# A trunk layer on one core: value weights of eight heads side by side, thirteen instead of ten seven-product pairs in the last matrix, and sums of its weights kept in DRAM

## The chip, the cores and the metric

The kernel runs on one core of one Trainium2 chip. The time is device microseconds of one execution of the whole layer. The kernel before takes 1129.91 us, the median of three runs from 1128.61 to 1129.95.

## The reference

One layer on x of 256 rows by 2048, in float32, with float32 weights. What the change touches is the value part of the first projection and the last product of the feed-forward part.

```python
h   = RMSNorm(x);  q, k, v = h @ w_in               # 16 heads of 128
o   = 8 stick-breaking heads | 8 dilated heads, each RMS-normalised
x   = x + RMSNorm(o @ w_out)                        # 2048 -> 2048
h   = RMSNorm(x)
u   = h @ w_up                                      # 2048 -> 2 x 5504
u   = sum(up[:, j:j + S] * conv_w[j] for j in range(3)) + conv_b
y   = gelu(gate) * val                              # 5504
out = x + RMSNorm(y @ w_down)                       # 5504 -> 2048
```

## The kernel before

**Weights.** All of them are float32 in DRAM and are used once. A chunk is 128 rows by 2048 columns, 1 MB, and is loaded by SP's queue in two pieces of 128x1024 (512 KB, function load, L78) into five slots called raw that go round: a load waits on SP until the slot's last reader is done, and everything behind it on SP waits with it. Each piece is split in two: ACT casts it to a rounded high part (wh, L88), VectorE (DVE) subtracts this from the piece and gets the low part (wl, L93; called "its low" below). Four buffers each hold wh and wl. TensorE (PE) then makes three matmuls of a product: high of the data by high of the weights, low by high, high by low. Loads run two chunks ahead of PE, the splits one.

**Order of chunks.** Four times: the four value chunks of four heads (kind "v", 2 PSUM banks), then eight chunks of queries and keys ("qk"). Then 16 chunks of "out", 86 of "up", and down. The first chunks are written out by hand: x comes transposed in pieces (load_x, L209) between the weights, and split_x makes its two parts. x for the residual, the tables and the parameters are loaded before chunks 4 to 7 (the table named between). The attention of each head runs in four or five steps beside the following chunks, its PSUM in the pool ps_at; chunks use ps_mm. A scheduler sets each engine's order from the program, except where pin keeps the written one (start, end, and the passage from out to up).

**Down.** y has 43 blocks of 128 columns of y (row blocks of w_down). The output is made in two halves of 1024 columns (cp 0 and 1), each in eight PSUM banks, numbered 1 to 8 by what is summed in them. A single row block takes four products (2 blocks of 128 rows of x by 2 blocks of 512 columns). A pair of row blocks is a 2x2 by 2x2 block product in seven products in the manner of Winograd; the weights' side needs the units T13 (two products), T24 (two), Rb (two, the plain blocks b11 and b22) and Ra (one, the plain block b21). With b12, b21 and [b11|b22] loaded, T13 is [b12|b12] + [b11|b22] (L542), and the two halves of T24 are the first of T13 plus b22 (L543) and this plus b21 (L544). Each unit then has its cast and its low, three units ahead of PE (AHEAD). The data's side (seven sums of y for each pair) is made during up in convolved. There are ten pairs and 23 singles, in the order of _down_plan: of the first half two singles, then a pair and one or two singles in turn, four singles at the end; of the second half the same without the two. The last four singles of the second half (HELD) are worked through bank by bank, and the final normalisation runs beside them, its order pinned: close adds a bank to its sum, rows.mean and newton make the row's factor, put multiplies, adds x and stores.

Of the kernel before, what the change touches and what calls it, by code (L numbers as in the profile page):

```python
# [9 lines left out]
F32 = mybir.dt.float32  # L10
# [6 lines left out]
P = 128  # L17
# [15 lines left out]

NPAIR = 10
HELD = 4
# [16 lines left out]
def layer_kernel(ctx: ExitStack, tc: tile.TileContext, a, out: bass.AP):  # L52
# [137 lines left out]
    A.preload_act_table_set("natural_log_exp_and_others")  # L190
    gpre = cpool.tile([P, KT], F32, name="gpre")
    par = cpool.tile([P, P_END], F32, name="par")
# [5 lines left out]
    apool = phA.__enter__()  # L198
    cst = apool.tile([P, C_END - P], F32, name="cst", bufs=1)
    x1 = apool.tile([P, 2, D], F32, name="x1", bufs=1)  # L200
    x1_kept = nc.dram_tensor("x1_kept", (S, D), F32, kind="Internal").ap()
# [18 lines left out]
    nc.scalar.dma_start(gpre, a["par"][:, P_PRE:P_PRE + KT])  # L220
    warm = cpool.tile([P, 512], BF16, name="warm")
# [4 lines left out]
    w0 = chunks[0][3]  # L226
# [11 lines left out]
    split_x(1, 2)  # L238
    parts_of[0] += split(raws[0][1:2])
    split_x(2, 4)  # L240
    parts_of[0] += split(raws[0][2:3])
    nc.scalar.dma_start(ident, a["cst"][:, C_ID:C_END])
    for i in range(1, 4):
        load_x(4 * i, 4 * i + 4)
        raws[i] = load(chunks[i][3], chunks[i][4])
        split_x(4 * i, 4 * i + 4)
        if i == 1:
            parts_of[1] = split(raws[1])
    between[4] = (x1[:, 0, :], a["x"][0:P, :])
    between[5] = (x1[:, 1, :], a["x"][P:S, :])  # L250
    between[6] = (cst, a["cst"][:, 0:C_ID])
    between[7] = (par, a["par"])

# [133 lines left out]
    class Rows:  # L387
# [6 lines left out]
        def squares(self, ps, t, c):  # L394
            jk = wpool.tile([P, 512], BF16, tag="jks", name="jks", bufs=1)
            jk = jk[:, 0:ps.shape[-1]]
            pin(A.activation(jk, ps, AF.Square, accum_out=self.ss[:, t, c:c + 1]))
# [50 lines left out]
    def convolved(ps, p, s):  # L448
# [4 lines left out]
        V.tensor_tensor(u, u, r2B, op=ALU.mult)  # L453
        cv = phB.tile([P, S], F32, tag=f"cv{s}", name="cv")
        A.activation(cv, u, AF.Identity, scale=cw(2), bias=par[:, P_CB + f:P_CB + f + 1])  # L455
        V.scalar_tensor_tensor(cv[:, 1:], u[:, :S - 1], cw(1), cv[:, 1:], op0=ALU.mult, op1=ALU.add)
        V.scalar_tensor_tensor(cv[:, 2:], u[:, :S - 2], cw(0), cv[:, 2:], op0=ALU.mult, op1=ALU.add)
        if s == 0:
            A.activation(cv, cv, AF.Gelu_apprx_tanh)
            gate[0] = cv  # L460
        else:
            m, odd = p // (FT // NPAIR), p % (FT // NPAIR)
            if p in SINGLES:
                n = SINGLES.index(p)
                V.tensor_tensor(cv, gate[0], cv, op=ALU.mult)
                A.copy(yt[0][:, n, :], cv)
                V.tensor_tensor(yt[1][:, n, :], cv, yt[0][:, n, :].bitcast(F32), op=ALU.subtract)
                return
            if odd == 0:
                pair[0] = phB.tile([P, 8, P], F32, tag="pair", name="pair", bufs=1)  # L470
# [12 lines left out]
    class Down:  # L483
# [6 lines left out]
        PAIR = (  # L490
            ("T13", ((5, 3, 0), (7, 5, 512))),
            ("T24", ((6, 4, 0), (4, 2, 512))),
            ("Rb", ((1, 0, 0), (3, 6, 512))),
            ("Ra", ((2, 1, 0),)),
        )
        ONE = ((4, 1, 0), (3, 0, 512), (2, 0, 0), (8, 1, 512))

        def __init__(self):
            self.units, self.tiles = [], []
            for cp in range(2):  # L500
                at = 0
                for kind, j in _down_plan(cp):
                    first = len(self.tiles)
                    n = 2 if kind == "pair" else 1
                    for _ in range(n):
                        self.tiles.append(a["w_dn"][cp, :, at:at + 1024])
                        at += 1024
# [5 lines left out]
            self.raws, self.parts, self.sums = [], [], {}  # L513
            self.left = {}
# [5 lines left out]
            self.begun = set()  # L520

        def load(self, n):
            while len(self.raws) < min(len(self.tiles), n):
                raw = wpool.tile([P, HALF], F32, tag="raw", name="raw", bufs=RAW_BUFS, padded_shape=[P, HALF])
                nc.sync.dma_start(raw, self.tiles[len(self.raws)])
                self.raws.append(raw)

        def prepare(self, n):
            while len(self.parts) < min(len(self.units), n):
                cp, what, j, first, _ = self.units[len(self.parts)]  # L530
                self.load(first + 5)
                ra = self.raws[first]
                if what == "one":
                    src = ra
                else:
                    rb = self.raws[first + 1]
                    if what == "T13":
                        t13, t24 = room[:, 3, 0:HALF], room[:, 3, HALF:]
                        self.sums = {"T13": t13, "T24": t24, "Rb": rb, "Ra": ra[:, 512:]}
                        b12 = ra[:, 0:512].rearrange("p (o c) -> p o c", o=1).broadcast_to([P, 2, 512])  # L540
                        two = lambda x: x.rearrange("p (o c) -> p o c", o=2)
                        V.tensor_tensor(two(t13), b12, two(rb), op=ALU.add)  # L542
                        V.tensor_tensor(t24[:, 0:512], t13[:, 0:512], rb[:, 512:], op=ALU.add)  # L543
                        V.tensor_tensor(t24[:, 512:], t24[:, 0:512], ra[:, 512:], op=ALU.add)  # L544
                    src = self.sums[what]
                self.parts.append(low(src, high(src)))
# [38 lines left out]
        def run(self):  # L585
# [66 lines left out]
            r = rows.newton(*mean)  # L652
            for lo, hi in ((0, 256), (256, 1024), (1024, 1536), (1536, 2048)):
                put(1, lo, hi, r)
            pinned[0] = False

    down = Down()
    for i, (kind, p, s, _, w) in enumerate(chunks):
        parts = ahead(i, 0 if (kind, p, s) == ("out", 3, 3) else SPLITS)
        if kind == "v":  # L660
            if s == 0:
                mm["v"] = [ps_mm.tile([P, 512], F32, tag="mm", name="mmv") for _ in range(2)]
            mm_moving(mm["v"], parts, hT[0], hT[1], 4 * s, s == 0, s == 3)
            if s == 3:
                late = LATE if p == 0 else 0
        if kind in ("v", "qk") and late is not None:
            if late == 0:
                g = p // 4 if kind == "qk" else p
                if g == 0:
                    first_norm()  # L670
                vts[g] = apool.tile([P, 2, 512], F32, tag="vt", name="vt")
                for t in range(2):
                    A.activation(vts[g][:, t, :], mm["v"][t], AF.Copy, scale=rstd1[:, t:t + 1])
                late = None
# [229 lines left out]
```

## Time and profile before

| | |
|---|---|
| median of the runs | 1129.91 us (1128.61 to 1129.95) |
| profiled execution, its own time | 1130.5 us |
| its span | 1128.7 us |
| granted clock | 0.998 |
| PE, DVE, ACT busy | 99%, 76%, 57% |
| bytes moved | 216.86 MB, 192 GB/s over the span |
| attention and out, up, down | to about 400, 414 to 893, 894 to 1120 us |

PE is what the traces call TensorE's matmuls, PEld its loading of stationary data, which overlaps; DVE is VectorE, ACT ScalarE, POOL GpSimd, and SP the engine whose queue issues nearly all DMAs. Rows of a timeline read: start, duration, engine, line, operation, output<-input, shapes, number of instructions that were merged in the row, and in brackets how long the engine had been idle before and for whom it had waited. Busy time of a matmul is longer than the step from one to the next, since they overlap; steps are read from starts. A group's row gives the sum and the mean of one in ns.

### The profile page before, as it was taken

To read this page: it belongs to the slowest core of one execution; us is meant where nothing else is said; L and a number is where in the kernel's file an instruction comes from. 1 tells how busy PE (TensorE), PEld (TensorE's weight loads), DVE (VectorE), ACT (ScalarE), POOL (GpSimd) and SP (SyncE) were. 2 spreads that over 40 slices of the span, in tenths; PEclk is the share of its full clock that TensorE was granted. 3 is DMA by queue.
4 is the path that set the end of the run, shared out by engine and by line. 5 is a ranking of instruction groups with operands and counts; after the bars stand their busy time and mean duration, and the time that the engine had idled before them with its cause. 6 is when DMAs were issued, how large, how long until landed. Compare 5 with 4: busy or idle time off the path is not lost.

```text
span 1128.7 us, 16033 instructions
## 1 busy us (share of the span) xinstructions
PE 1112.2 (99%) x5873; PEld 945.2 (84%) x5873; DVE 857.0 (76%) x1340; ACT 646.6 (57%) x1039; POOL 3.6 (0%) x10
## 2 busy tenths in 40 slices
PE   8999999999999989999999999999999999999996
PEld 6888888888888878888888888888888878877885
DVE  6665565766765489788888887888888898888987
ACT  7555564655654386555555555555555555554653
POOL 0000000000000000000000000000000000000000
PEclk9999999999999999999999999999999999999999
DMA  9764545545555556555555555555555555555555
GB/s 357 251 209 164 180 157 168 168 155 181 166 169 188 187 186 206 186 187 187 186 188 187 187 189 186 188 186 189 187 188 187 162 206 205 205 199 205 202 198 204
DMA packets 59695, 216.86 MB, mean 192 GB/s; under 512 B 6753, under 2 KB 7393, under 8 KB 58849
## 3 DMA queue, kind: packets, MB, share of 16 engines
q1 hardware_dynamic: 59328, 215.77, 57.4%
q8 instruction: 46, 0.75, 0.3%
q14 instruction: 33, 0.26, 0.1%
q10 hardware_dynamic: 288, 0.07, 0.0%
HBM read 211.63 MB, written 4.19 MB: 191 GB/s over the span
## 4 chain that ended last, share of the span: by engine, by line
PE 95%; DVE 2%; ACT 1%; DMA 1%; issue 0%; SPq 0%; DVEq 0%; ACTq 0%
PE mmu L101 28%; PE mmu L104 14%; PE mmqk L101 10%; PE p L563 6%; PE p L561 6%; PE p L562 6%; PE mmqk L104 5%; PE mmo L138 3%; PE mmo L134 3%; PE mmo L135 3%; PE mmv L134 3%; PE mmv L135 2%; PE mmv L138 2%; DVE wl L93 1%; DMA mg<-in_xT 1%; PE mmu L111 1%
## 5 line engine op out<-in xcount | busy, mean ns | idle before, releaser
L93 DVE TENSOR_TENSOR wl<-raw,wh 128x1024 fp32r<-128x1024 f32 (+1 forms) x387 | 457.9, 1193 | 202.4 <-ACT wh L88 199.7
L88 ACT CAST wh<-raw 128x1024 fp32r<-128x1024 f32 (+1 forms) x387 | 394.4, 1027 | 342.7 <-PE mmu L101 194.5
L101 PE MATMUL mmu<-hT,wh 128*128 128x512 f32 x1344 | 340.6, 395 | 0.2 <-ACT wh L88 0.2
L101 PEld LDWEIGHTS mmu<-hT,wh 128*128 128x128 f32 x1344 | 240.8, 188 | 45.0 <-ACT wh L88 0.4
L104 PEld LDWEIGHTS mmu<-hT,wl 128*128 128x128 f32 x1344 | 184.1, 188 | 15.3
L104 PE MATMUL mmu<-hT,wl 128*128 128x256 f32 x1344 | 187.4, 282 | 0.0
L101 PE MATMUL mmqk<-hT,wh 128*128 128x512 f32 x512 | 132.9, 400 | 0.0
L101 PEld LDWEIGHTS mmqk<-hT,wh 128*128 128x128 f32 x512 | 92.0, 188 | 17.1
L88 ACT CAST wh<-room 128x1024 fp32r<-128x1024 f32 x40 | 42.0, 1050 | 71.1 <-DVE room L542 49.5
L104 PEld LDWEIGHTS mmqk<-hT,wl 128*128 128x128 f32 x512 | 70.0, 188 | 5.8
L561 PE MATMUL p<-wh,yt 128*128 128x512 f32 (+1 forms) x188 | 72.9, 388 | 0.0
L562 PE MATMUL p<-wh,yt 128*128 128x512 f32 (+1 forms) x188 | 72.9, 388 | 0.0
L563 PE MATMUL p<-wl,yt 128*128 128x512 f32 (+1 forms) x188 | 72.5, 386 | 0.2 <-DVE wl L93 0.2
L104 PE MATMUL mmqk<-hT,wl 128*128 128x256 f32 x512 | 71.2, 281 | 0.0
L561 PE MATMUL p<-wh,yp 128*128 128x512 f32 x140 | 55.2, 395 | 0.4 <-ACT wh L88 0.4
L563 PE MATMUL p<-wl,yp 128*128 128x512 f32 x140 | 54.6, 394 | 0.5 <-DVE wl L93 0.5
L562 PE MATMUL p<-wh,yp 128*128 128x512 f32 x140 | 55.0, 393 | 0.0
L134 PE MATMUL mmv<-wh,hT 128*128 128x512 f32 x128 | 51.7, 405 | 1.6 <-ACT wh L88 1.3
L455 ACT ACTIVATE cv<-u,par 128x256 f32<-128x256 f32 x86 | 51.4, 598 | 2.1 <-DVE u L453 2.1
L93 DVE TENSOR_TENSOR wl<-room,wh 128x1024 fp32r<-128x1024 f32 x40 | 48.9, 1222 | 4.4 <-ACT wh L88 3.6
L135 PE MATMUL mmv<-wh,hT 128*128 128x512 f32 x128 | 50.7, 396 | 0.3 <-DVE hT L236 0.3
L134 PE MATMUL mmo<-wh,mix 128*128 128x512 f32 x128 | 50.6, 396 | 0.0
(175 smaller groups left out, 1219.1 us busy)
## 6 DMA issues: line engine op xcount, KB each, us to landing
raw<-in_w_up SPq DMA_DIRECT2D x172, 512.0 KB, 4.4
raw<-in_w_dn SPq DMA_DIRECT2D x86, 512.0 KB, 4.3
raw<-in_w_qk SPq DMA_DIRECT2D x64, 512.0 KB, 3.7
raw<-in_w_o SPq DMA_DIRECT2D x32, 512.0 KB, 3.6
raw<-in_w_v SPq DMA_DIRECT2D x31, 512.0 KB, 3.8
x<-in_x SPq DMA_DIRECT2D x2, 1024.0 KB, 9.3
x_kept<-x SPq DMA_DIRECT2D x2, 1024.0 KB, 4.4
x1b<-x_kept SPq DMA_DIRECT2D x4, 512.0 KB, 5.4
```

Source lines behind the costliest of these rows:

```text
L88: pin(A.copy(wh, raw))
L93: pin(V.tensor_tensor(wl, raw, wh.bitcast(F32), op=ALU.subtract))
L101: T.matmul(ps, wh[:, j * P:(j + 1) * P], h[:, k, :, :], start=(k == 0), stop=False, skip_group_check=True)
L104: T.matmul(ps[:, 0, :], wl[:, j * P:(j + 1) * P], h[:, k, 0, :], start=False, stop=(k == KT - 1), skip_group_check=True)
L111: T.matmul(ps[:, 0, :], w[:, k % 8 * P:(k % 8 + 1) * P], h[:, k, 0, :], start=(k == 0 and w is parts[0][0]), stop=False, skip_group_check= ...
L134: T.matmul(ps[t], hi[:, k, tc_], ws, start=(first and i == 0 and j == 0), stop=False)
L135: T.matmul(ps[t], lo[:, k, tc_], ws, start=False, stop=False)
L138: T.matmul(ps[t], hi[:, k, tc_], wl[:, j * 512:(j + 1) * 512], start=False, stop=(last and i == len(parts) - 1 and j == n - 1))
L455: A.activation(cv, u, AF.Identity, scale=cw(2), bias=par[:, P_CB + f:P_CB + f + 1])
L561: T.matmul(ps, yh, wh[:, cs], start=key not in self.begun, stop=False)
L562: T.matmul(ps, yl, wh[:, cs], start=False, stop=False)
L563: T.matmul(ps, yh, wl[:, cs], start=False, stop=self.left[key] == 0)
```

## The change

1. **Pairs.** NPAIR goes from 10 to 13, so there are 17 singles. In down there is now one single between two pairs (none behind pairs 0 and 6 of the first half). On the data's side one of the eight sums is written in place, so that seven lie together and take one cast and one subtraction instead of two each; the row numbers in PAIR follow.
2. **Sums ahead of time.** A new function, presum, makes T13 of all 26 pair tiles during attention and out, one per two chunks, from chunk 8 to 61: SP loads b12 (256 KB) and [b11|b22] (512 KB), two chunks later DVE adds them, one chunk after that SP stores the sum (512 KB) in DRAM (t13_kept). Down loads T13 from there, and [b11|b22] and b21 (256 KB) from the weights: three tiles for a pair instead of two, and no sum of T13 in down. The two sums of T24 go to alternate halves of the last quarter of room.
3. **Start.** The value chunks of the first two groups of four heads alternate, with the second group's PSUM taken from ps_at, then come the 16 query and key chunks of eight heads. The loads of x, the tables and the parameters move from chunks 4 to 7 to chunks 8 to 11. The vectors vt of both groups are made together.
4. **End.** The put of 512 columns of row block 0 is cut in two with rows.mean between, and the last multiplication by the gain (take9) moves behind the first two puts of row block 1.
5. **Buffers.** Some tiles go to other pools or to single buffers (gpre, warm, u, cv, jks).

```diff
-NPAIR = 10
+NPAIR = 13
...
-        u = pool.tile([P, S], F32, tag=name, name=name)
+        u = pool.tile([P, S], F32, tag=name, name=name, bufs=1)
...
-    for g in range(4):
+    for gs in ((0, 1), (2,), (3,)):
         for kq in range(4):
-            chunks.append(("v", g, kq, a["w_v"][g, kq], 2048))
-        for h in range(4 * g, 4 * g + 4):
+            for g in gs:
+                chunks.append(("v", g, kq, a["w_v"][g, kq], 2048))
+        for h in range(4 * gs[0], 4 * gs[-1] + 4):
...
     raws[0] += load(w0[:, 0:512], 512)
     load_x(0, 2)
     raws[0] += load(w0[:, 512:1024], 512)
+    raws[1] = load(w1[:, 0:1024], 1024)
     load_x(2, 4)
     raws[0] += load(w0[:, 1024:], 1024)
+    raws[1] += load(w1[:, 1024:], 1024)
...
-    between[4] = (x1[:, 0, :], a["x"][0:P, :])
+    between[8] = (x1[:, 0, :], a["x"][0:P, :])
...
-                a11, a21, a12, a22, s1, s2, s3, s4 = (y[:, j, :] for j in range(8))
+                a11, a21, a12, a22, s1, s2, s4 = (y[:, j, :] for j in range(7))
                 V.tensor_tensor(s1, a22, a21, op=ALU.subtract)
-                V.tensor_tensor(s3, a11, a21, op=ALU.subtract)
+                V.tensor_tensor(a21, a11, a21, op=ALU.subtract)
...
-                for dst, src in ((slice(0, 1), slice(0, 1)), (slice(1, 7), slice(2, 8))):
-                    A.copy(yp[0][:, m, dst, :], y[:, src, :])
-                    V.tensor_tensor(yp[1][:, m, dst, :], y[:, src, :], yp[0][:, m, dst, :].bitcast(F32), op=ALU.subtract)
+                A.copy(yp[0][:, m, :, :], y)
+                V.tensor_tensor(yp[1][:, m, :, :], y, yp[0][:, m, :, :].bitcast(F32), op=ALU.subtract)
...
+                    if kind == "pair":
+                        self.tiles += [kept[cp, j], a["w_dn"][cp, :, at + 1024:at + 2048], a["w_dn"][cp, :, at + 512:at + 1024]]
+                        self.presums.append((a["w_dn"][cp, :, at:at + 512], self.tiles[-2], kept[cp, j]))
...
+        def presum(self, tick):
+            pair, odd = divmod(tick, 2)
+            if odd and self.summed and tick > 2:
+                t13, _, kept = self.summed.pop(0)
+                nc.sync.dma_start(kept, t13)
+            if not odd and self.summed:
+                t13, one, _ = self.summed[0]
+                b12 = one.rearrange("p (o c) -> p o c", o=1).broadcast_to([P, 2, 512])
+                two = t13.rearrange("p (o c) -> p o c", o=2)
+                V.tensor_tensor(two, b12, two, op=ALU.add)
+            if not odd and pair < len(self.presums):
+                one, two, kept = self.presums[pair]
+                b12 = apool.tile([P, 512], F32, tag="b12", name="b12")
+                nc.sync.dma_start(b12, one)
+                t13 = apool.tile([P, HALF], F32, tag="t13", name="t13")
+                nc.sync.dma_start(t13, two)
+                self.summed.append((t13, b12, kept))
...
-                        V.tensor_tensor(two(t13), b12, two(rb), op=ALU.add)
+                    rb, b21 = self.raws[first + 1], self.raws[first + 2]
+                    if what == "T24":
+                        t24 = room[:, 3, j % 2 * HALF:(j % 2 + 1) * HALF]
                         V.tensor_tensor(t24[:, 0:512], t13[:, 0:512], rb[:, 512:], op=ALU.add)
-                        V.tensor_tensor(t24[:, 512:], t24[:, 0:512], ra[:, 512:], op=ALU.add)
+                        V.tensor_tensor(t24[:, 512:], t24[:, 0:512], b21, op=ALU.add)
...
-            put(0, 1536, 2048, r)
+            put(0, 1536, 1792, r)
             mean = rows.mean(1, 5)
+            put(0, 1792, 2048, r)
+            r = rows.newton(*mean)
+            put(1, 0, 256, r)
+            put(1, 256, 1024, r)
             pin(take9(V))
...
+        if 8 <= i < 62:
+            down.presum(i - 8)
...
+                pool, tag = (ps_at, "at") if p == 1 else (ps_mm, "mm")
+                mm["v", p] = [pool.tile([P, 512], F32, tag=tag, name="mmv") for _ in range(2)]
```

What the scheduler makes of it shows in the order of instructions. First DVE in down, around a pair in the middle of the first half; before, L542 to L544 are the three sums, "wl<-room" the lows of T13 and T24, "wl<-raw" those of Rb, Ra (128x512) and the singles:

```order
L542 TENSOR_TENSOR room<-raw 128x1024
L543 TENSOR_TENSOR room<-room,raw 128x512
L544 TENSOR_TENSOR room<-room,raw 128x512
L93 TENSOR_TENSOR wl<-room,wh 128x1024 x2
```

and after the change, with the sums of T24 at L569 and L570 and T13 read from a raw slot:

```order
L569 TENSOR_TENSOR room<-raw 128x512
L570 TENSOR_TENSOR room<-room,raw 128x512
L93 TENSOR_TENSOR wl<-room,wh 128x1024
L93 TENSOR_TENSOR wl<-raw,wh 128x1024
L93 TENSOR_TENSOR wl<-raw,wh 128x512
L93 TENSOR_TENSOR wl<-raw,wh 128x1024 x2
L569 TENSOR_TENSOR room<-raw 128x512
L570 TENSOR_TENSOR room<-room,raw 128x512
```

The low of T24 now always stands straight behind its own second sum; before, the low of T13 stood between in most pairs. Between one pair's second sum and the next pair's first stand five lows: T24, Rb, Ra, the single and the next T13.

Second PE, in the same place after the change: p6, p4, p1 and p3 are PSUM banks, L588 is high by high, L589 low by high, L590 high by the weights' low. T24 feeds banks 6 and 4, Rb 1 and 3.

```order
L588 MATMUL p6_9005<-wh_9262,yp0_4084 128x512
L589 MATMUL p6_9005<-wh_9262,yp1_4085 128x512
L588 MATMUL p4_9007<-wh_9262,yp0_4084 128x512
L589 MATMUL p4_9007<-wh_9262,yp1_4085 128x512
L588 MATMUL p1_9006<-wh_9269,yp0_4084 128x512
L589 MATMUL p1_9006<-wh_9269,yp1_4085 128x512
L590 MATMUL p6_9005<-wl_9264,yp0_4084 128x512
L590 MATMUL p4_9007<-wl_9264,yp0_4084 128x512
```

The two matmuls by T24's low stand behind six by high parts; before, each stood right behind the two of its own bank.

Third SP at the start, before and then after. x in pieces is mg<-in_xT.

```order
L78 DMA raw<-in_w_v 128x512
L209 DMA mg<-in_xT 128x512
L78 DMA raw<-in_w_v 128x512
L209 DMA mg<-in_xT 128x512
L78 DMA raw<-in_w_v 128x1024
L209 DMA mg<-in_xT 128x1024
```

```order
L78 DMA raw<-in_w_v 128x512
L210 DMA mg<-in_xT 128x512
L78 DMA raw<-in_w_v 128x512
L78 DMA raw<-in_w_v 128x1024
L210 DMA mg<-in_xT 128x512
L78 DMA raw<-in_w_v 128x1024 x2
```

A piece of weights of the second group comes ahead of the second piece of x.

More of the change, by code (lines that the diff above doesn't have):

```diff
@@ L244, in layer_kernel @@
         load_x(4 * i, 4 * i + 4)
-        raws[i] = load(chunks[i][3], chunks[i][4])
+        for j in range(2 * i, 2 * i + 2):
+            raws[j] = load(chunks[j][3], chunks[j][4])
         split_x(4 * i, 4 * i + 4)
         if i == 1:
-            parts_of[1] = split(raws[1])
-    between[4] = (x1[:, 0, :], a["x"][0:P, :])
-    between[5] = (x1[:, 1, :], a["x"][P:S, :])
-    between[6] = (cst, a["cst"][:, 0:C_ID])
-    between[7] = (par, a["par"])
+            parts_of[2] = split(raws[2])
+    between[8] = (x1[:, 0, :], a["x"][0:P, :])
+    between[9] = (x1[:, 1, :], a["x"][P:S, :])
+    between[10] = (cst, a["cst"][:, 0:C_ID])
+    between[11] = (par, a["par"])
     negones = apool.tile([P, P], F32, name="negones", bufs=1)
@@ L469, in convolved @@
             if odd == 0:
-                pair[0] = phB.tile([P, 8, P], F32, tag="pair", name="pair", bufs=1)
+                pair[0] = phB.tile([P, 7, P], F32, tag="pair", name="pair", bufs=1)
             y = pair[0]
@@ L531, in prepare @@
                 self.load(first + 5)
-                ra = self.raws[first]
+                t13 = self.raws[first]
                 if what == "one":
-                    src = ra
+                    src = t13
                 else:
[L536 to L542, printed above, removed]
+                    rb, b21 = self.raws[first + 1], self.raws[first + 2]
+                    if what == "T24":
+                        t24 = room[:, 3, j % 2 * HALF:(j % 2 + 1) * HALF]
                         V.tensor_tensor(t24[:, 0:512], t13[:, 0:512], rb[:, 512:], op=ALU.add)
-                        V.tensor_tensor(t24[:, 512:], t24[:, 0:512], ra[:, 512:], op=ALU.add)
-                    src = self.sums[what]
+                        V.tensor_tensor(t24[:, 512:], t24[:, 0:512], b21, op=ALU.add)
+                        self.t24 = t24
+                    src = {"T13": t13, "T24": self.t24, "Rb": rb, "Ra": b21}[what]
                 self.parts.append(low(src, high(src)))
@@ L648, in run @@
             put(0, 1280, 1536, r)
[L649 removed]
+            put(0, 1536, 1792, r)
             mean = rows.mean(1, 5)
+            put(0, 1792, 2048, r)
+            r = rows.newton(*mean)
+            put(1, 0, 256, r)
+            put(1, 256, 1024, r)
             pin(take9(V))
[L652 to L654 removed]
+            put(1, 1024, 1536, r)
+            put(1, 1536, 2048, r)
             pinned[0] = False
@@ L659, in layer_kernel @@
         parts = ahead(i, 0 if (kind, p, s) == ("out", 3, 3) else SPLITS)
+        if 8 <= i < 62:
+            down.presum(i - 8)
         if kind == "v":
             if s == 0:
[L662 to L665, printed above, removed]
+                pool, tag = (ps_at, "at") if p == 1 else (ps_mm, "mm")
+                mm["v", p] = [pool.tile([P, 512], F32, tag=tag, name="mmv") for _ in range(2)]
+            if i == 0:
+                pass
+            elif i == 1:
+                for half in range(2):
+                    for g in range(2):
+                        some = parts_of[g][2 * half:2 * half + 2] if g == 0 and half == 0 else parts_of[g][half - 2:][:1]
+                        mm_moving(mm["v", g], some, hT[0], hT[1], 2 * half, half == 0, False)
+            else:
+                mm_moving(mm["v", p], parts, hT[0], hT[1], 4 * s, s == 0, s == 3)
+            if s == 3 and p > 0:
+                late = LATE if p == 1 else 0
         if kind in ("v", "qk") and late is not None:
             if late == 0:
-                g = p // 4 if kind == "qk" else p
-                if g == 0:
+                gs = (0, 1) if kind == "qk" else (p,)
+                if gs == (0, 1):
                     first_norm()
-                vts[g] = apool.tile([P, 2, 512], F32, tag="vt", name="vt")
-                for t in range(2):
-                    A.activation(vts[g][:, t, :], mm["v"][t], AF.Copy, scale=rstd1[:, t:t + 1])
+                for g in gs:
+                    vts[g] = apool.tile([P, 2, 512], F32, tag="vt", name="vt")
+                    for t in range(2):
+                        A.activation(vts[g][:, t, :], mm["v", g][t], AF.Copy, scale=rstd1[:, t:t + 1])
                 late = None
```

32 lines of the change are left out of this document (18 added, 14 removed).

## The prediction

> **What bounds the kernel now.** I began with the totals of the page and the share of the chain of waits by engine.
>
> ```profile
> span 1128.7 us, 16033 instructions
> PE 1112.2 (99%) x5873; PEld 945.2 (84%) x5873; DVE 857.0 (76%) x1340; ACT 646.6 (57%) x1039; POOL 3.6 (0%) x10
> PE 95%; DVE 2%; ACT 1%; DMA 1%; issue 0%; SPq 0%; DVEq 0%; ACTq 0%
> ```
>
> TensorE is busy 99% of the span and holds 95% of the chain. So the time can fall in two ways only: fewer matmuls, or less of the little idling that is left. Next came the stages, one window each (length, busy time of PE, its weight loads, DVE, ACT and POOL, granted clock, DMA share, GB/s).
>
> ```profile
> 0.00:20.00 20.00, 16.90 (x61) 10.75 (x62) 12.96 (x22) 13.78 (x23) 0.86 (x7) 1.00 0.90 332
> 14.00:20.00 6.00, 6.00 (x27) 4.82 (x27) 6.00 (x9) 5.75 (x11) 0.00 (x0) 1.00 1.03 425
> 20.00:60.00 40.00, 39.80 (x213) 33.50 (x212) 26.37 (x42) 23.88 (x33) 0.51 (x1) 1.00 0.79 286
> 110.00:157.00 47.00, 47.00 (x280) 41.50 (x279) 28.34 (x47) 26.22 (x49) 0.00 (x0) 1.00 0.52 168
> 205.00:236.00 31.00, 31.00 (x186) 27.37 (x185) 22.27 (x50) 20.50 (x49) 0.00 (x0) 1.00 0.52 167
> 424.00:890.00 466.00, 466.00 (x2650) 406.81 (x2649) 381.73 (x626) 270.57 (x417) 0.00 (x0) 1.00 0.58 189
> 894.00:1120.00 226.00, 224.84 (x985) 182.09 (x983) 202.79 (x220) 127.25 (x150) 1.18 (x1) 1.00 0.57 198
> ```
>
> Attention and up leave PE no gap, up with DVE at 82% (381.73 of 466). Idle time is left in the first 20 us and in down, where DVE is at 90% (202.79 of 226). The clock is full throughout. The list of what PE waited for names the releasers: the first row is of 0 to 20 us, the others of down.
>
> ```profile
> PE mmv L134 <- ACT wh L88: 1.3, 2, 0.7
> PE p L563 <- DVE wl L93: 0.8, 2, 0.5
> PE p L561 <- ACT wh L88: 0.4, 2, 0.3
> ```
>
> **The change part by part.** The sum is made against the profiled execution, 1130.5 us (span 1128.7 and 1.8 around it); the median shown is 1129.91, 0.6 lower.
>
> *Eighteen matmuls less.* Three more pairs, each with seven products for eight, two column halves, three matmuls a product: 18. The price is from the chain, which gives each matmul of 512 columns the same step, and the length of down from its first and last matmul.
>
> ```profile
> 1116.79 0.23 PE p L562
> 1117.03 0.23 PE p L563
> L561 PE MATMUL p<-wh,yt x188: 279/392/398, 893.8 to 1119.6; 128*128 128x512 f32 x180, 128*128 128x256 f32 x8
> L563 PE MATMUL p<-wl,yt x188: 276/388/505, 894.3 to 1119.8; 128*128 128x512 f32 x180, 128*128 128x256 f32 x8
> ```
>
> 18 x 0.23 = **-4.1 us**. Down now has 328 products of three matmuls, 24 of these matmuls at half width: 972 full widths, 223.6 us, in a stretch from 893.8 to 1119.9 (the last start and half a step), 226.1. So PE loses **2.5 us** to waits in down.
>
> *Waits in down.* This is the term that decides. DVE sets the pace of a pair, as its timeline shows.
>
> ```profile
> 962.73 1.22 DVE L93 TENSOR_TENSOR wl<-room,wh 128x1024 fp32r<-128x1024 f32 x1
> 963.87 0.69 DVE L544 TENSOR_TENSOR room<-room,raw 128x512 f32<-128x512 f32 x1
> 965.75 1.23 DVE L93 TENSOR_TENSOR wl<-room,wh 128x1024 fp32r<-128x1024 f32 x1 [1.19 <-ACT wh L88]
> 966.89 4.09 DVE L93 TENSOR_TENSOR wl<-raw,wh 128x1024 fp32r<-128x1024 f32 x4
> 971.86 1.23 DVE L542 TENSOR_TENSOR room<-raw 128x1024 f32<-128x1024 f32 x1 [0.88 <-DMA raw<-in_w_dn]
> 973.12 0.69 DVE L543 TENSOR_TENSOR room<-room,raw 128x512 f32<-128x512 f32 x1
> 973.85 0.69 DVE L544 TENSOR_TENSOR room<-room,raw 128x512 f32<-128x512 f32 x1
> L542 DVE TENSOR_TENSOR room<-raw 128x1024 f32<-128x1024 f32 x20 | 24.5, 1223 | 11.7 <-DMA raw<-in_w_dn 10.2 <-PE mmu L104 1.5
> L93 DVE TENSOR_TENSOR wl<-raw,wh 128x512 fp32r<-128x512 f32 x22 | 15.1, 688 | 0.0
> ```
>
> By starts, a full low takes 1.14 (962.73 to 963.87), the first T24 sum 0.73 (973.12 to 973.85). Where the second sum has its cast straight behind it, as it always will, 1.88 pass up to the low (963.87 to 965.75), 1.19 of it waiting for ACT. A half low takes 0.69 less the 0.09 by which busy time exceeds the step of a full one: 0.60. A pair and one single then cost DVE 0.73 + 1.88 + T24 1.14 + Rb 1.14 + Ra 0.60 + single 1.14 + T13 of the next 1.14 = **7.77 us**. PE needs 33 matmuls, 7.59. DVE is behind by 0.18 a step. A pair without a single (pairs 0 and 6 of the first half) costs 6.62 against 21 matmuls, 4.83. Before, most pairs had two singles (45 matmuls, 10.35), and DVE's longer pair (1.23 more for L542, and 10.2 us over twenty pairs waiting for a DMA) had room beside it. The first half runs eleven steps between pair 1 and the last, ten of 7.77 and one of 6.62, 84.3, where PE has 80.7; less 0.3 of slack from the singles ahead, PE waits 3.3. The second half starts with some 1.7 of slack (a single is 2.76 for PE and 1.14 for DVE, and the first half ends on four; how far DVE may run ahead is limited by four buffers) and takes 86.0 where PE has 83.5: 0.8. Together 4.1 for 2.5: **+1.6**. Bounds: no wait left, -2.5; and 0.15 more a step over 22 steps, +4.9. I take the sum of the rows, nearest to the work.
>
> *One tile more a pair, loaded late.* The order on SP gives the block b21 the slot that Rb frees. From the end of Rb's low to the second sum of the next pair DVE has 0.60 + 1.14 + 1.14 + 0.69, about 3.5 us. The nearest rows are a 512 KB tile in such a slot, from its issue to the instruction that waited for it, and the landing times of down's loads.
>
> ```profile
> 978.12 0.33 SPq L525 DMA_DIRECT2D raw<-in_w_dn  x1
> 981.61 1.23 DVE L542 TENSOR_TENSOR room<-raw 128x1024 f32<-128x1024 f32 x1 [0.64 <-DMA raw<-in_w_dn]
> DMA to landing us min/median/max: 3.3/4.3/6.4
> ```
>
> 3.49 us for 512 KB; 256 KB fewer at 425 GB/s (first windows) is 0.6 less, 2.9: **0**. Bounds: 0, and a tile that takes the median's 4.3 less 0.6, 0.2 late in each of 22 steps, 4.4. I take 0: its like took 3.49, not 4.3. The Trainium skill, DMA: Bandwidth & Descriptors, section "Latency and other measured facts", speaks against it: it gives HBM access as 0.2 us on average and 2 us at high load. By that, an estimate, 2.9 could become 4.7, 1.2 us late. The landings of down, 3.3 to 6.4 for one size, agree that the spread is of that order.
>
> *Sums made in attention.* 26 adds of 1.22 (L542's mean) are 31.8 us of DVE over some 340, 9 points on top of 60% (28.34 of 47) to 72% (22.27 of 31); up ran at 82% without a gap. The bytes, 768 KB read and 512 KB written a pair, 34 MB in all, add 100 GB/s to 168; in 14 to 20 us the queues moved 425 GB/s while PE was busy 6.00 of 6.00. Each add stands two chunks behind its loads and one ahead of its store, so neither DVE nor SP, behind which the weights wait, should stop. **0**; if that cover fails, a store that holds SP costs up to a DVE step, 0.25 of PE for each of 26, **+6.5**.
>
> *Start.* PE's two long waits:
>
> ```profile
> 6.12 0.62 ACT L88 CAST wh<-raw 128x512 fp32r<-128x512 f32 x1 [0.59 <-DMA raw<-in_w_v]
> 8.72 1.05 ACT L88 CAST wh<-raw 128x1024 fp32r<-128x1024 f32 x1 [1.07 <-DMA raw<-in_w_v]
> 8.72 0.39 PE L138 MATMUL mmv<-wl,hT 128*128 128x512 f32 x1
> 9.82 0.50 PE L134 MATMUL mmv<-wh,hT 128*128 128x512 f32 x1 [0.70 <-ACT wh L88]
> 12.25 0.63 PE L138 MATMUL mmv<-wl,hT 128*128 128x512 f32 x2
> 13.48 0.50 PE L134 MATMUL mmv<-wh,hT 128*128 128x512 f32 x1 [0.60 <-ACT wh L88]
> ```
>
> 8.72 + 0.23 to 9.82 is 0.87; 12.25 + two steps to 13.48 is 0.77; 1.64 in all. After the change the next 512 KB of weights need no new x. Between 6.12 and 8.72 landed 768 KB, so 512 KB take 1.73: there at 7.85, cast by 8.90, and PE is free at 8.95. From then on each x piece feeds two groups. I leave 0.2 of the waits: **-1.45** (bounds 0, if x comes as late, and -1.64). x1 and the tables come four chunks later; they are what the 425 GB/s carried without a gap.
>
> *Up.* Pairs, row sums and single buffers add under 10 us to DVE's 381.73 of 466, so at most 84%: **0**, hidden behind PE.
>
> *Tail.*
>
> ```profile
> 1120.45 1.13 DVE L620 SCALAR_TENSOR_TENSOR room<-room,rs,x1p 128x256 f32<-128x256 f32 x2
> 1121.50 0.15 DVE L407 TENSOR_SCALAR_CACHE_REDUCE rj<-ssd 128x5 f32<-128x5 f32 x1
> 1121.58 0.42 DVE L583 TENSOR_TENSOR room<-room 128x256 f32<-128x256 f32 x1
> 1122.61 2.74 DVE L620 SCALAR_TENSOR_TENSOR room<-room,rs,x1b 128x256 f32<-128x256 f32 x4
> ```
>
> The mean (L407) stands behind a put of half the width, some 0.25 earlier, but the multiply by the gain (L583), which was covered by ACT's logarithm, now stands among the last puts, 0.4: **+0.15** (bounds -0.25 and +0.4).
>
> Sum: -4.1 + 1.6 + 0 + 0 - 1.45 + 0 + 0.15 = **-3.8**: 1126.7 by the profiled execution, **1126.1** by the median.
>
> **The rivals.** *PE alone sets down* (waits fall to 0.5, -2.0 for +1.6): 1122.5. For it: 10.2 us of DVE's waits on DMA go, and AHEAD = 3 units of lead absorb single late steps. Against: a lead is spent when every step is 0.18 long, and 7.77 came from rows without a semaphore's extra. *DVE's step is longer than the rows say*, by 0.15 (a T24 cast queued behind another on ACT, a single's load): 22 x 0.15 = 3.3, 1129.4, no measurable change. For it: nothing is left to cover ACT's cast, and PE issues T24's lows six matmuls behind its highs. Against: ACT is at 56% in down (127.25 of 226). *The late b21*: from a landing above 3.5 us DVE stops in each step; half a microsecond late is 22 x 0.5 = 11 us, 1137, slower. For it: the landings of 3.3 to 6.4. Against: half the bytes. *The store in attention holds the weights back*: +6.5, 1132.6, slower. For it: SP sends in order. Against: the add is done a chunk before. That the start's order does nothing is a rival of the start term alone: 1127.5, inside the forecast's own range.
>
> **How the numbers follow.** Forecast 0.44, PE alone 0.14, longer step 0.24, late b21 0.10, store 0.08. 0.2% of 1130 is 2.3 us, about what a measurement can tell: faster is below 1127.6. The forecast and PE alone are faster, but of the forecast 0.02 lies above that bound: 0.56. The longer step and that 0.02 make 0.26 the same; the last two 0.18 slower. The forecast's own range is 1124 to 1128. The whole range begins where no wait is left in down and the start gains all (-4.1 - 2.5 - 1.64 + 0.15, 1121.8) and takes in the store's 1132.6; outside is the late tile alone.
>
> **What would show it.** In the changed profile: 18 matmuls fewer in down; PE's waits for L88 in the first 15 us below 0.3 in all; DVE above 95% busy or waiting for casts from pair to pair with a period near 7.8 us, and PE's matmuls spread to it; no row of L570 waiting for a DMA; windows of attention with PE at full length and some 270 GB/s. It would be wrong if the period from one first sum to the next is 7.6 or less (PE alone) or 8.0 and more (longer step, or with a DMA beside L570 the late tile), or if SP's stores show waits while PE has gaps between 60 and 390 us.

## The result and the profile after

The changed kernel is slower: 1139.08 us, median of six runs from 1135.03 to 1145.99, against 1130.22 for the kernel before beside it; the ratio is 1.008, with a 95% interval of 1.0059 to 1.010. The forecast was 1126.1, the range 1121.8 to 1132.6. The profiled execution of the changed kernel took 1137.48. Its page:

```profile
span 1135.7 us, 16294 instructions
PE 1113.2 (98%) x5855; PEld 939.6 (83%) x5855; DVE 880.2 (78%) x1370; ACT 652.8 (57%) x1038; POOL 3.6 (0%) x10
GB/s 345 321 277 287 289 308 283 316 338 324 213 168 187 194 169 215 191 186 187 187 190 183 193 186 190 186 186 185 187 187 188 181 231 227 229 239 223 244 229 231
```

PE has the 18 matmuls less and is nevertheless busy longer. The traffic of the sums is drawn together in the slices 2 to 10, where some 300 GB/s flow, not 270 up to 390 us. Split by the first matmul of up, the first and the last of down and the end, the two profiled executions differ so (us):

| stage | before | after | difference | forecast |
|---|---|---|---|---|
| start, attention, out: to the first matmul of up | 403.5 | 412.0 | +8.5 | -1.45 |
| up | 490.3 | 490.3 | 0 | 0 |
| down: first to last matmul | 226.1 | 224.8 | -1.3 | -2.5 |
| tail | 8.8 | 8.5 | -0.3 | +0.15 |

By the profiles the kernel is 7.0 us longer where 3.8 fewer were forecast. Of these 10.8 some 10.0 are in the first stage and 1.2 in down; the tail is 0.4 better than forecast. The windows of the first stage (columns as before):

```profile
110.00:157.00 47.00, 43.97 (x264) 38.54 (x263) 32.59 (x59) 27.11 (x64) 0.00 (x0) 1.00 0.87 295
157.00:205.00 48.00, 44.33 (x218) 36.41 (x217) 30.16 (x49) 22.99 (x41) 0.00 (x0) 0.96 0.88 292
175.00:180.00 5.00, 2.67 (x12) 1.75 (x12) 4.90 (x12) 2.29 (x4) 0.00 (x0) 0.97 1.00 355
180.00:184.00 4.00, 4.00 (x12) 3.13 (x11) 0.41 (x2) 0.61 (x2) 0.00 (x0) 0.61 0.85 304
```

PE, which was busy throughout both stretches before, is idle for 3.0 and 3.7 us in the first two. After the gaps between 175 and 180 us its granted clock is 0.61 in the mean of 4 us: 0.50 from 179.73 to 183.14 and 1.00 around that, which costs another 1.7 (half of 3.41). The lists of what PE, DVE and SP waited for, the last two from 60 to 400 us:

```profile
PE z L355 <- DVE spl L352: 5.2, 4, 2.1
PE pt L329 <- DVE on L325: 1.5, 2, 1.2
```

```profile
DVE t L542 <- DMA t<-in_w_dn: 16.0, 10, 3.6
```

```profile
SPq L548 <- DMA t_kept<-t: 30.1, 13, 5.2
```

L355 and L329 are steps of the heads' attention, L542 is presum's add, L548 its load of [b11|b22]. The timeline of the largest gap connects them:

```profile
111.81 0.33 SPq L548 DMA_DIRECT2D t<-in_w_dn  x1
113.70 0.50 ACT L350 CAST sph<-sp 128x384 fp32r<-128x384 f32 x1
116.43 0.42 PE L354 MATMUL z<-sph,tri 128*128 128x384 f32 x1
117.25 1.23 DVE L542 TENSOR_TENSOR t<-b,t 128x1024 f32<-128x1024 f32 x1 [3.52 <-DMA t<-in_w_dn]
118.39 0.55 DVE L352 TENSOR_TENSOR spl<-sp,sph 128x384 fp32r<-128x384 f32 x1
119.00 0.44 PE L355 MATMUL z<-spl,tri 128*128 128x384 f32 x1 [2.15 <-DVE spl L352]
```

The load went out at 111.81, after SP had waited 2.7 us for the store that had to empty its buffer. DVE had come to the add 3.52 us before the load landed, and stood. Behind the add stood spl (L352), an operand of PE's next matmul: its inputs were there at 114.20, when ACT's cast (L350) ended, but it began at 118.39, behind the add, and PE's matmul came 2.15 late.

The first half of down goes as the prediction had it, step for step. DVE:

```profile
942.22 0.68 DVE L569 TENSOR_TENSOR room<-raw 128x512 f32<-128x512 f32 x1
942.94 0.69 DVE L570 TENSOR_TENSOR room<-room,raw 128x512 f32<-128x512 f32 x1
944.82 1.22 DVE L93 TENSOR_TENSOR wl<-room,wh 128x1024 fp32r<-128x1024 f32 x1 [1.19 <-ACT wh L88]
949.97 0.68 DVE L569 TENSOR_TENSOR room<-raw 128x512 f32<-128x512 f32 x1
956.59 0.68 DVE L569 TENSOR_TENSOR room<-raw 128x512 f32<-128x512 f32 x1
```

From first sum to first sum 7.75 us with a single (forecast 7.77) and 6.62 without (forecast 6.62), with 1.19 of waiting for T24's cast in each.

### The profile page after: what moved, and what is told of

It reads as the page before. It is cut to its first block, busy times and chain, and to the rows that moved or that the text cites. A ratio compares the mean times of both kernels' runs of the same rounds, so it can differ in the third digit from the quotient of the medians.

```text
span 1135.7 us, 16294 instructions
## 1 busy us (share of the span) xinstructions
PE 1113.2 (98%) x5855; PEld 939.6 (83%) x5855; DVE 880.2 (78%) x1370; ACT 652.8 (57%) x1038; POOL 3.6 (0%) x10
## 4 chain that ended last, share of the span: by engine, by line
PE 78%; DVE 3%; ACT 1%; issue 1%; DMA 0%; DVEq 0%; ACTq 0%
PE mmu L101 28%; PE mmu L104 14%; PE p L588 5%; PE p L590 5%; PE mmqk L101 5%; PE p L589 5%; PE mmqk L104 3%; PE mmo L134 3%; PE mmo L135 3%; PE mmo L138 3%; DVE wl L93 1%; PE mmv L134 1%; PE mmv L135 1%; PE mmv L138 1%; PE mmu L111 1%
## 5 line engine op out<-in xcount | busy, mean ns | idle before, releaser
L93 DVE TENSOR_TENSOR wl<-raw,wh 128x1024 fp32r<-128x1024 f32 (+1 forms) x413 | 482.9, 1186 | 165.0 <-ACT wh L88 160.0
L88 ACT CAST wh<-raw 128x1024 fp32r<-128x1024 f32 (+1 forms) x413 | 414.6, 1021 | 335.1 <-PE mmu L101 190.0
L588 PE MATMUL p<-wh,yp 128*128 128x512 f32 x182 | 73.9, 406 | 1.7 <-ACT wh L88 1.7
L88 ACT CAST wh<-room 128x1024 fp32r<-128x1024 f32 x26 | 27.2, 1048 | 81.2 <-DVE room L570 67.9
L589 PE MATMUL p<-wh,yp 128*128 128x512 f32 x182 | 71.5, 393 | 0.0
L590 PE MATMUL p<-wl,yp 128*128 128x512 f32 x182 | 64.0, 393 | 0.0
L93 DVE TENSOR_TENSOR wl<-room,wh 128x1024 fp32r<-128x1024 f32 x26 | 31.9, 1225 | 28.8 <-ACT wh L88 25.2
L590 PE MATMUL p<-wl,yt 128*128 128x512 f32 (+1 forms) x140 | 54.0, 387 | 0.0
L588 PE MATMUL p<-wh,yt 128*128 128x512 f32 (+1 forms) x140 | 54.0, 386 | 0.0
L589 PE MATMUL p<-wh,yt 128*128 128x512 f32 (+1 forms) x140 | 53.7, 385 | 0.0
```

Of the source, the lines that this page charges most:

```text
L88: pin(A.copy(wh, raw))
L93: pin(V.tensor_tensor(wl, raw, wh.bitcast(F32), op=ALU.subtract))
L588: T.matmul(ps, yh, wh[:, cs], start=key not in self.begun, stop=False)
L589: T.matmul(ps, yl, wh[:, cs], start=False, stop=False)
L590: T.matmul(ps, yh, wl[:, cs], start=False, stop=self.left[key] == 0)
```

## The experiments

The ratios are against the kernel before on the same chip, 1130.1 to 1130.5 in the three groups.

| run | median us | ratio, 95% interval |
|---|---|---|
| changed kernel | 1139.08 | 1.0080, 1.0059 to 1.0100 |
| no presum, T13 unsummed | 1127.63 | 0.9974, 0.9965 to 0.9984 |
| presum without its add | 1127.59 | 0.9972, 0.9961 to 0.9983 |
| presum in program order | 1127.90 | 0.9978, 0.9969 to 0.9987 |
| presum on GpSimd | 1140.54 | 1.0100, 1.0072 to 1.0129 |
| start alone, on the kernel before | 1129.73 | 0.9989, 0.9979 to 0.9998 |
| program order, ten pairs | 1126.40 | 0.9963, 0.9950 to 0.9976 |
| program order, T24 in halves | 1132.30 | 1.0014, 1.0001 to 1.0028 |
| no presum, sums in down | 1136.33 | 1.0046, 1.0029 to 1.0062 |
| program order, T24's sums ahead of T13's low | 1126.13 | 0.9967, 0.9955 to 0.9979 |
| the same with twelve pairs | 1125.44 | 0.9960, 0.9947 to 0.9973 |
| program order, T24 in halves, order of down held | 1121.44 | 0.9924, 0.9912 to 0.9937 |

**What in attention costs the time.** Three theories: DVE stands at the add; SP, standing at the load, holds the weights back; or the bytes slow the weights. The first run leaves all of presum out:

```diff
-                        self.tiles += [kept[cp, j], a["w_dn"][cp, :, at + 1024:at + 2048], a["w_dn"][cp, :, at + 512:at + 1024]]
+                        self.tiles += [a["w_dn"][cp, :, at + 1024:at + 2048], a["w_dn"][cp, :, at + 1024:at + 2048], a["w_dn"][cp, :, at + 512:at + 1024]]
...
-        if 8 <= i < 62:
-            down.presum(i - 8)
```

> Of the changed kernel, the sums in attention are left out altogether (presum isn't called; down takes the unsummed block [b11|b22] where T13 stood, so T13 and T24 are not the sums they should be). Down has the same loads, sums of T24, casts and matmuls as the changed kernel. Theories: the loss lies in attention alone (PE stops at steps of the heads between 100 and 215 us, 8.4 us, and its clock falls once, some 1.6 us): then PE has no such waits, and the time is 1139 less about 10 to 12, 1127 to 1129. Rival: the loss is elsewhere too (start, up or down): 1133 or more.

1127.63, as expected of a loss in attention alone: without presum the changed kernel is 11.5 us faster than with it, and no wait of PE at a head's step is left. The second run takes the add alone away:

```diff
-                V.tensor_tensor(two, b12, two, op=ALU.add)
```

> Of the changed kernel, only VectorE's add of presum is left out: the loads of b12 and [b11|b22] and the stores stay, so that what is kept in DRAM is the unsummed block. Theory DVE: VectorE works in order and stands at the add until its load has landed (16.0 us over 60 to 400 us), and the heads' steps behind it come late: then PE's waits at the heads' steps go, and the time is 1127 to 1130. Theory SP: the load of presum waits on SP for the store of the pair before last (30.1 us) and holds the weights behind it: then the time stays near 1139, with PE waiting for casts. Theory bytes: 34 MB more slow the weights: it stays near 1139 too, with SP's waits for the store still there.

1127.59, as without presum. Loads and stores were all there, and SP waited longer than in the changed kernel:

```profile
SPq L547 <- DMA t_kept<-t: 59.5, 21, 5.7
```

So 59.5 us in which SP stood at presum's load (L547 here), and all the bytes, 322 to 351 GB/s between 110 and 205 us, cost PE nothing: the theories SP and bytes fall. The third run keeps the add and holds the order:

```diff
-                nc.sync.dma_start(kept, t13)
+                tc.keep_in_program_order(nc.sync.dma_start(kept, t13))
```

and likewise for the add and the two loads.

> The changed kernel with presum's loads, adds and stores held in program order on SP and VectorE: four pieces of weights between one pair and the next on SP, where the changed kernel has two or three. Theory DVE (the scheduler drew the pairs together, so that two buffers of T13 turn every 9 us and each load is late): the load's lead grows, VectorE's waits at the add fall from 16 us to under 4, the time is 1128 to 1132. Theory bytes: the same bytes over 330 us instead of 240: 1132 to 1136. Theory SP: SP's waits for the store fall too, 1128 to 1132; only the run without the add tells it from DVE.

1127.90. The adds of the changed kernel and of this run, and SP's waits and the first of the windows in this run:

```profile
L542 DVE TENSOR_TENSOR t<-b,t x26: 1216/1224/1227, 56.7 to 288.0; 128x1024 f32<-128x1024 f32 x26
```

```profile
L542 DVE TENSOR_TENSOR t<-b,t x26: 1214/1216/1220, 65.5 to 378.7; 128x1024 f32<-128x1024 f32 x26
```

```profile
SPq L537 <- DVE t L542: 39.8, 26, 3.9
SPq L548 <- DMA t_kept<-t: 28.2, 20, 3.8
110.00:157.00 47.00, 47.00 (x287) 41.75 (x286) 33.67 (x66) 29.41 (x67) 0.00 (x0) 1.00 0.76 256
```

The scheduler had drawn the 26 adds together, one per 9.3 us instead of 12.5. The ring of two buffers (load, add, store, next load) then turned so fast that loads were late. In program order DVE never waits at the add, SP waits 68 us at the stores and loads of presum, and PE loses nothing. Why the scheduler drew them together isn't settled by a run, and no run has a third buffer. The 26 adds themselves, 31.6 us of DVE, cost 0.3 us beside the run without presum, within the intervals.

The fourth run moved all of presum to GpSimd, the loads and stores to its queue:

```diff
-                V.tensor_tensor(two, b12, two, op=ALU.add)
+                tc.keep_in_program_order(G.tensor_tensor(two, b12, two, op=ALU.add))
```

> The changed kernel with presum whole on GpSimd: its loads and stores from GpSimd's queue, the add on GpSimd, in program order. SP and VectorE carry nothing of it; the bytes are the same. Theories DVE and SP: no gap of PE in attention, 1126 to 1129. Theory bytes: 1134 or more. A new price may show: GpSimd's add of 128x1024 (by the tail's row of two 128x512 in 2.19 us some 2.2 us) beside VectorE.

1140.54: the expectation was wrong, by a cost that none of its theories had, though it had said that a new price might show. The profiled execution is the longest of the four, 1147.11 at a mean clock of 0.992; the others took 1140.00 to 1140.85 at 0.996 to 0.998. Groups of DVE between 60 and 300 us, of the run in program order and of this one, and this one's first wait of PE:

```profile
L93 DVE TENSOR_TENSOR wl<-raw,wh 128x1024 fp32r<-128x1024 f32 x75 | 91.8, 1224 | 55.7 <-ACT wh L88 54.8
L728 DVE TENSOR_TENSOR qk<-mmqk,half 128x256 f32<-128x256 f32 x29 | 12.1, 418 | 0.0
L368 DVE TENSOR_TENSOR qk<-qk,rot 128x512 f32<-128x512 f32 x7 | 4.8, 686 | 0.0
```

```profile
L93 DVE TENSOR_TENSOR wl<-raw,wh 128x1024 fp32r<-128x1024 f32 x70 | 101.8, 1458 | 50.0 <-ACT wh L88 47.4 <-PE mmqk L104 2.4
L728 DVE TENSOR_TENSOR qk<-mmqk,half 128x256 f32<-128x256 f32 x27 | 11.2, 415 | 0.0
L368 DVE TENSOR_TENSOR qk<-qk,rot 128x512 f32<-128x512 f32 x5 | 7.7, 1547 | 0.0
PE z L372 <- DVE qk L368: 8.0, 5, 2.3
```

Beside GpSimd's adds DVE's own instructions take longer: a low 1.46 instead of 1.22, L368 1.55 instead of 0.69, and PE waits for L368. Two rivals, GpSimd's adds and its DMA issues, are told apart by the single instructions of the trace. Between 60 and 300 us 24 lows of 128x1024 overlap an add: the 9 that began before it took 1.22 to 1.23 us, and the 15 that began during it ended 1.08 to 1.16 us after the add's end, whenever they had begun, so they stood until the add was done. The 11 that overlap a DMA issue of GpSimd alone took 1.21 in the mean. The instructions with one input in PSUM (L728, L325, L332, L348) are as before, those that overlap an add too.

**What the parts bring.** The start alone (the hunks of the chunk list, of the first loads and of the loop):

```diff
-    for g in range(4):
+    for gs in ((0, 1), (2,), (3,)):
```

> The kernel before with the start of the change alone: the value chunks of eight heads side by side and the four later loads. Theory: PE's two long waits of the first 14 us shrink to one short one and nothing else moves; forecast of the prediction -1.45, from the two traces of the changed kernel without gaps the attention ends 1.7 us earlier: 1128.5 to 1129. Rival: what the start gains, the later loads or the longer row of query chunks take back: 1130.4.

1129.73, between what was expected and the rival: 1.2 us better by the ratio, 0.2 to 2.4 by its interval. Then ten pairs with the sums ahead, in program order:

```diff
-NPAIR = 13
+NPAIR = 10
```

> The changed kernel with presum in program order and ten pairs instead of thirteen. Theory DVE (VectorE sets the pace of down with thirteen pairs): with ten, most pairs have two singles, VectorE needs 7.75 + 1.14 = 8.9 us where PE needs 10.3, PE's waits in down vanish; 18 more matmuls cost 4.1, the waits saved are 4 to 5: 1126 to 1128, not slower than with thirteen pairs (1127.9). Rival: the matmuls alone count: 1132.

1126.40, not slower than thirteen pairs with 1127.90, though it has 18 matmuls more. What three pairs save on PE they lose again to DVE's pace: by the profiles down takes 225.3 us with ten pairs and 225.0 with thirteen. Last, thirteen pairs without presum: Down's tiles and sums are those of the kernel before.

```diff
+                        V.tensor_tensor(two(t13), b12, two(rb), op=ALU.add)
                         V.tensor_tensor(t24[:, 0:512], t13[:, 0:512], rb[:, 512:], op=ALU.add)
```

> The changed kernel without presum: thirteen pairs, but T13 is made in down from two tiles of 512 KB, as in the kernel before. Theory DVE: a pair took 6.75 us of VectorE before, and 0.5 of waiting for a load; with one single 8.4, where PE has 7.59 and the changed kernel 7.75. Over 22 steps that is 14 us more than with the sums ahead: 1142, between 1131 (no wait for loads) and 1155. Rival (the sums ahead don't matter in down): 1128.

1136.33, with down at 232.9 us where it was 225.0. A step took 7.88, not the 8.4 expected: the low of T13 stood where DVE otherwise waits 1.19 for T24's cast. So of each sum of 1.22 that presum takes out of down, a step got 0.13; over 22 steps 2.9 us. The other 5 lie mostly in the first pairs of each half; that the sum stands there in the chain to PE's first matmul is likely, but was not tested.

**What sets down's pace.** If it is DVE with its wait for the cast, shortening that must help. Cast and low of T24 in two halves, the order left to the scheduler:

```diff
+                    for h in (slice(0, 512), slice(512, HALF)):
+                        A.copy(wh[:, h], src[:, h])
+                        V.tensor_tensor(wl[:, h], src[:, h], wh[:, h].bitcast(F32), op=ALU.subtract)
```

> The changed kernel with presum in program order; T24's cast and low are each made in two halves of 512 columns, so that the first half is cast while VectorE makes the second sum. Theory DVE: the 1.19 us in which VectorE waits for the cast go, two halves cost 0.1 to 0.2 more than a whole, a pair with a single takes about 6.8 us, less than PE's 7.59: PE's waits in down go, 1123 to 1124.5. Rival (the waits come from ACT, or from the loads of down): 1127 to 1129.

1132.30: worse than without it, and than the rival of its expectation. The wait for the cast is gone (2.2 us in all of down), but the scheduler moved the first sum ahead of the lows of T13 and the single, and DVE now stands there for the load:

```profile
DVE room L569 <- DMA raw<-in_w_dn: 25.7, 21, 1.9
```

That is the late tile of the prediction's rivals, though with another block. Two runs separate the halves from the order. In the first the cast is whole and both sums stand ahead of T13's low, so that b21 has 2.4 us from slot to use instead of 3.5:

```diff
+                wh = high(src)
+                if what == "T13":
+                    t24 = room[:, 3, j % 2 * HALF:(j % 2 + 1) * HALF]
+                    self.chain(lambda: V.tensor_tensor(t24[:, 0:512], t13[:, 0:512], rb[:, 512:], op=ALU.add))
+                    self.chain(lambda: V.tensor_tensor(t24[:, 512:], t24[:, 0:512], b21, op=ALU.add))
```

chain holds the order of these instructions on DVE (tc.issue_after).

> The changed kernel with presum in program order, and in down both sums of T24 moved ahead of T13's low on VectorE (order held there: sum, sum, low of T13, T24, Rb, Ra, single): the low of T13 stands where VectorE waited 1.19 us for T24's cast. Theory DVE: a step with one single shrinks from 7.75 to about 6.6 us; the block b21 is needed 1.14 earlier, 2.4 us after its slot comes free, where a quarter of a megabyte needed some 2.9, so perhaps 0.5 of waiting for it: 7.1, still under PE's 7.57. Down goes from 225.0 to 219.5 to 221, the time to 1122.5 to 1124. Rival late tile: the wait for b21 takes what the cast gave back, 1.1 or more, period 7.7 or more: 1127 to 1129.

1126.13 by the median, between the expectation and its rival. The profiled execution took 1123.01 with down at 220.5, as expected; the runs spread up to 1128.69. The profile shows the late b21, and more of it than a step can bear at times:

```profile
DVE room L572 <- DMA raw<-in_w_dn: 12.3, 18, 1.8
```

That the slower executions have longer waits of this kind is likely but was not seen, as the profile is of the fastest. The second run has the halves with the changed kernel's order held on DVE and ACT; the run in program order has this order on DVE without the halves:

```diff
+                step = 512 if what == "T24" else w
+                for c in range(0, w, step):
+                    h = slice(c, c + step)
+                    self.chain(lambda: A.copy(wh[:, h], src[:, h]), 1)
+                    self.chain(lambda: V.tensor_tensor(wl[:, h], src[:, h], wh[:, h].bitcast(F32), op=ALU.subtract))
```

> As the run with T24's cast and low in halves, but with VectorE's sums and lows and ACT's casts of down held in the changed kernel's order, so that the first sum isn't moved ahead of T13's and the single's lows, and each block's time from slot to use stays as in the changed kernel. Theory (the run without that order lost its gain because the first sum stood 25.7 us waiting for its load): no wait for loads beside the sums, a step of 6.7 to 6.9 us, under PE's 7.57, down 219.5 to 221, the time 1122.5 to 1124. Rival (halves cost PE or ACT something of their own): 1128 or more.

1121.44, from 1121.41 to 1121.59 in all four runs: 0.8% faster than the kernel before. The window of down and DVE's step:

```profile
892.00:1111.00 219.00, 219.00 (x970) 179.44 (x969) 201.50 (x250) 139.32 (x186) 0.74 (x1) 1.00 0.71 237
```

```profile
951.50 0.68 DVE L569 TENSOR_TENSOR room<-raw 128x512 f32<-128x512 f32 x1
952.22 0.69 DVE L570 TENSOR_TENSOR room<-room,raw 128x512 f32<-128x512 f32 x1
952.95 1.34 DVE L580 TENSOR_TENSOR wl<-room,wh 128x512 fp32r<-128x512 f32 x2
958.57 0.68 DVE L569 TENSOR_TENSOR room<-raw 128x512 f32<-128x512 f32 x1
```

Here 7.07 us pass from sum to sum, and in most of the second half 7.55, which is PE's own step, 33 matmuls at 0.229: there DVE goes at PE's pace. PE has no gap, and down takes 218.8 us. The mean step of down's matmuls that follow one another without a wait in the kernel before is 0.2294, and 954 of these are 218.9. The step is longer than the 6.7 to 6.9 expected, and the time is under the 1122.5 to 1124. Only here do the 18 matmuls count in full. The check by number of pairs:

> The first run of this call with twelve pairs: six matmuls more, 1.4 us, and more singles between pairs. If VectorE no longer sets the pace with thirteen, this is 1.4 slower than that run; if it still does, the same or faster.

1125.44 with twelve, within the intervals of thirteen: it decides nothing, since the run with thirteen pairs itself lost time to the late tile.

## Why the prediction was wrong

**The step that failed** is in *Sums made in attention*: "Each add stands two chunks behind its loads and one ahead of its store, so neither DVE nor SP, behind which the weights wait, should stop." That is the order in which the program is written. The built order was another: between one pair and the next SP had mostly two or three pieces of weights, not four. In the gap shown, DVE came to the add at 113.73 (3.52 before 117.25), only 1.9 us after its load had gone out at 111.81; these loads take 3.5 to 7.0 us to land. The term was 0 and measures +11.2 us (1139.08 against 1127.90 in program order). By the profiles it is 10.6: PE reaches up at 412.0, in program order at 401.4. Seven waits add up to 8.4 by starts, 1.7 is the lower clock (3.41 us at 0.50), and 0.5 is spread over smaller ones.

The bound for this term, +6.5, was too small too, because it came from the wrong mechanism. The rival "the store in attention holds the weights back" had the place and the sign, and a chance of 0.08. The prediction's last sign of being wrong, SP's waits beside gaps of PE between 60 and 390 us, did come. But the run without the add refutes the rival as a cause: SP stood for 59.5 us and PE lost nothing. The weights are loaded far enough ahead; what has no lead is a head's step behind an add in DVE's order. I had asked who waits behind SP, but not who waits behind the add on DVE. With program order the term is 0.3, within the intervals of the 0 that was forecast.

**Down.** In the first half the pace of DVE was right to 0.02 us a step, and so was the theory that it decides. The mis-sized term is that of PE's waits: +1.6, with bounds of -2.5 and +4.9. With 0.2294 a matmul, PE waits 5.9 us after the change and 3.1 before, +2.8. The first half has the forecast's 3.3 and 0.2 more; the second has 2.4 where I had 0.8. These 0.8 were too much by the prediction's own rows: eleven steps of 7.77 are 85.5, not 86.0, which leaves 0.3. Three steps of the second half take 8.2 us instead of 7.75. In two of them multiplications by the gain of the first half's banks (take in the code) stand on DVE between the two sums, so that the order of the middle of the first half doesn't hold there:

```profile
1028.77 0.68 DVE L569 TENSOR_TENSOR room<-raw 128x512 f32<-128x512 f32 x1
1029.37 0.68 DVE L610 TENSOR_TENSOR room<-room 128x512 f32<-128x512 f32 x1
1029.97 0.68 DVE L570 TENSOR_TENSOR room<-room,raw 128x512 f32<-128x512 f32 x1
```

I had left them out of the cycle. In the third DVE waits for b21, the only time in the changed kernel:

```profile
DVE room L570 <- DMA raw<-in_w_dn: 0.5, 1, 0.5
```

Each of the three is some 0.45 longer, 1.4 together; most of the slack of 1.7 went into them.

**Late b21.** The term 0 held but for that one wait of 0.5 us. That the margin was as narrow as the rival said is shown by the run that took 1.14 of it away: 18 waits. By the 2 us of HBM access at high load that the Trainium skill gives in DMA: Bandwidth & Descriptors, section "Latency and other measured facts", b21 would have come 1.2 us past the window (the prediction's estimate); one wait in 26 pairs does not agree with that.

**Start.** -1.45 was forecast. PE's wait for the weights' cast fell from two of 1.3 us together to one of 0.3, and by the times the start alone brings 1.2, 0.2 to 2.4; its forecast lies inside this interval. **Tail.** +0.15 was forecast, -0.3 measured. **Up.** 0 and 0.

**The sum.** With the order mended, the changed kernel takes 1127.90, 2.5 better than before by the ratio, where the forecast had 3.8. The 1.3 between lie in down's waits (1.2) and within the intervals of the rest.

## What to carry to other kernels

Work that is put beside a full engine must be read in the order that the scheduler built, on each engine that runs in order: look at what stands behind the new instruction, and count the lead of its operands in that order, not in the program's. A ring of few buffers that is turned faster than its transfers come makes them late (10 of 26 adds had to wait here), and holding the program's order can be the whole cure. And before matmuls are saved, ask whether PE is what sets the pace there: thirteen pairs were no faster than ten (1127.90 against 1126.40) until DVE's wait for a cast was taken out, which brought 6.5 us and put them 4 to 5 ahead. Ten pairs without that wait were not run.

## What the runs showed of the hardware

In the changed kernel two gaps of PE of 1.40 and 1.34 us, which end at 177.17 and 178.94, were followed by a granted clock of 0.50 for 3.41 us; a single gap of 2.39 us (116.43 to 119.00, less 0.18 for the matmul itself) left it at 1.00. The same gaps need not do the same: behind the passage from out to up, whose first gap is 1.54 or 1.55 us, the clock was 0.50 for 3.41 us in the runs with ten pairs and with T24 in halves and the order held, and 1.00 in the kernel before, the changed kernel and the run in program order. So short waits can cost more than their length, and unevenly: the changed kernel's runs go from 1135.0 at a mean clock of 0.998 to 1146.0 at 0.994. Of these 11 us the clock is some 4.6 (an estimate, 0.004 of 1140); the rest is not explained. The Trainium skill, TensorE: Matmul & The Clock Gate, section "What's actually happening", tells of a clock that is halved after an idle window of about 3.4 us; the drop agrees in kind, but no gap before it in attention was that long.

GpSimd's add of 128x1024, 2.6 us between 60 and 300 us, held up DVE's instructions with two inputs in SBUF that began during it: a low ended 1.08 to 1.16 us after the add, whenever it had begun. A low that began first ran its 1.22 us, and the add beside it took 2.46 to 3.38 us, where an add that began beside none of these took 2.38 to 2.41. DVE's instructions with one input in PSUM were not held up (L728, 418 and 415 ns). That agrees with the Trainium skill, SBUF — State Buffer, section "Who interferes with whom", by which a DVE instruction with two inputs in SBUF contends with a GpSimd instruction that reads SBUF, the later one waiting until the earlier is done. A step of 128x2 with a single tensor input in SBUF (L316) was held up too: it began 0.05 us behind an add and took 2.38 us instead of 0.16.
